# Holding the tensor engine's instructions to the order of the file, in a two-layer trunk on one Trainium2 core

## The chip, the core and the metric

The kernel runs on one core of a Trainium2 chip. The metric is the device time of one execution in microseconds (us). The engines are named as the profile names them: PE is TensorE (PEld its weight loads), DVE is VectorE, ACT is ScalarE, POOL is GpSimd, and SP is the engine that issues the transfers. PEclk is the clock that TensorE was granted, as a share of 2.4 GHz.

## What is computed

A trunk of two layers over 256 positions of width 1024. Layer 0 mixes tokens by dilated attention (16 heads of 64, three key groups), layer 1 by an mLSTM block (inner width 2048, four heads, two chunks of 128). Each layer also has a squared-ReLU MLP and a gated per-layer embedding. Cut to what matters here:

```
# every layer i:
x += mixer_i(rms_norm(x));  x += W2 relu(W1 rms_norm(x))^2
x += sigmoid(rms_norm(x) @ W_g) * (p[i] @ W_p)
# layer 0: q, k = rms_norm(q), rms_norm(k) per head, before the scores
# layer 1, per head: the running maximum m, then
s   = (q @ k.T) * exp(d_mat - m_t)
num = sc * (q @ C) + s @ v
den = sc * (q @ n) + sum(s)
h   = num / max(|den|, exp(-m_t))      # then an RMS norm of h over the head
```

## The kernel before

The activations live in SBUF with features on the partitions and the 256 positions along the free axis. All large weights are streamed from HBM once, as units of 1 MB (`raw`, three buffers). ACT rounds each chunk of 512 columns to `hi` (line 180, in `split`), DVE forms `lo = raw - hi` (line 181), and a product in full precision is three matmuls on PE: high by high, low by high, high by low. In the attention's projections (`qkv_block`, lines 487 to 519) these have 512 columns (lines 503 to 505), in `stream` (lines 335 to 337) 256.

The program is written against a clock of slots, four to a unit. `open_slot` and `close_slot` frame a slot's matmuls, 12 of them in either kind of stage, which is what a later step's due time counts in. `at(slot, f)` puts small work (norms, transposes, scores, the mLSTM's per-head steps) behind the matmuls of a slot. That is the order of the file. The framework's scheduler may reorder what stands in it on each engine: it takes, of the instructions that its own model holds to be ready, the one of highest priority, so that a matmul whose input that model holds to be late is put back and others go ahead of it. Each engine then executes its list strictly in order.

The places that matter:

- `qkv_block`: a block of queries and keys takes 8 slots, two halves (`b` is the half of the positions) of eight k-steps each. Behind it `qk_stats` (a reduction, line 438) and `qk_norm` (lines 442 to 447) run on DVE: a reciprocal root of some ten small dependent instructions (`rsqrt`, lines 285 to 289), then two wide products into `nqk` (line 447). `TQ` slots later `qk_turn` transposes `nqk` on PE (line 455).
- `first_stats` (added at slot 0) computes the very first norm's statistics, `rx`, with another `rsqrt` on DVE; `Stats.total` forms `ssum` (line 273) and sums it over partitions on PE (line 276).
- `small_products` (lines 405 to 424): at slot 44 a transfer on SP brings `rep` (in the buffer `pj`), and POOL forms small products of weights from it (lines 415 to 421), used much later in the mLSTM.
- `spread` (lines 291 to 298): DVE writes a diagonal `dg` from a column (line 295), PE multiplies it by ones (line 297), ACT copies the result (line 298).
- the mLSTM's per-head steps, at slots that `HS` and `HO` set (line 203): `decay`, `memory`, `factor` and `merge`. `factor` (lines 900 to 913) sums `s1` (shown as `s`) on PE (line 903), runs 14 small dependent DVE instructions (lines 905 to 908 and 285 to 289), and calls `spread`, whose `dg` PE needs. `memory` of the next head needs `p`, which `decay` makes on DVE (lines 870 and 871). `merge` (lines 915 to 926) is wide work on DVE.
- `scores` (lines 522 to 537) issues the products of two heads pairwise into two PSUM buffers; DVE's reduction of a buffer (line 544) frees it.

Of the kernel before, what the change touches and what calls it, by code (L numbers as in the profile page):

```python
# [18 lines left out]
D, S, P = 1024, 256, 128  # L19
# [113 lines left out]
def build(tc, a):  # L133
    nc = tc.nc
    ctx = ExitStack()
    with ctx:
        _build(ctx, tc, nc, a)


def _build(ctx, tc, nc, a):  # L140
# [16 lines left out]

    act = nc.scalar.activation
    dve = nc.vector
    mm = nc.tensor.matmul  # L160


    raw, hi, lo = {}, {}, {}
# [39 lines left out]
    GT, HS, HO = (4, 6, 7), (6, 12, 18, 24), (0, 2, 5, 7)  # L203
    ST0 = 3.5
    ST1 = 1
    TQ = 4

    TA = (12, 7)

    def at(slot, f, *args):  # L210
        fill.setdefault(slot, []).append((f, args))
# [19 lines left out]
    ident = base.tile([P, P], F32, name="ident")  # L231
# [17 lines left out]
    def pr(n):  # L249
        o, w = PCOL[n]  # L250
        return prm[:, o:o + w]
# [31 lines left out]
    def rsqrt(y, v, shape):  # L283
        t = sqp.tile(shape, F32, name="rt")
        dve.tensor_scalar(y.bitcast(I32), v.bitcast(I32), -0.5, RSQRT_MAGIC, op0=ALU.mult, op1=ALU.add)
        for _ in range(3):
            dve.tensor_tensor(t, y, y, op=ALU.mult)
            dve.scalar_tensor_tensor(t, t, -0.5, v, op0=ALU.mult, op1=ALU.mult)
            dve.scalar_tensor_tensor(y, t, 1.5, y, op0=ALU.add, op1=ALU.mult)
# [88 lines left out]
    def first_stats():  # L378
        st.total()
        sw = atp.tile([P, P], F32, name="sw")  # L380
        dve.tensor_copy(sw[:, 0:64], st.s[:, 192:256])
        dve.tensor_copy(sw[:, 64:128], st.s[:, 0:64])
        for n, t in ((2, st.s[:, 64:192]), (3, sw)):
            mm(st.ps[:, 256 + n:257 + n], t, ones[:, 0:1], start=True, stop=True)
        v = atp.tile([P, 4], F32, name="v4")
        dve.tensor_scalar(v, st.ps[:, 256:260], 1.0 / D, EPS, op0=ALU.mult, op1=ALU.add)
        dve.tensor_scalar(epsx, v[:, 0:2], EPS, None, op0=ALU.mult)
        rsqrt(rx, v, [P, 4])
# [3 lines left out]
            act(hW[n][:, :, 0:64], hA[n][:, :, 192:256], AF.Copy)  # L392
            act(hW[n][:, :, 64:128], hA[n][:, :, 0:64], AF.Copy)

    at(0, first_stats)
    at(8, wrap)


# [1 line left out]
    rep = pj.rearrange("p a b -> p (a b)")[:, 0:NR]  # L400
# [2 lines left out]
    wgM = base.tile([P, 16, 8], F32, name="wgM")  # L403

    def small_products():
        nc.sync.dma_start(rep, a["rep"])
        wq, wk, wv = (pr(n).rearrange("p (k j) -> p k j", j=4) for n in ("wq", "wk", "wv"))
        t2 = atp.tile([P, 16, 8], F32, name="t2")

        def contract(out, w, name, n, add=None):  # L410
            o, c = RCOL[name]
            r = rep[:, o:o + c].rearrange("p (k n j) -> p k n j", n=n, j=4)
            t = atp.tile([P, 16, 8, 4], F32, name="ct")[:, :, :n]
            for k in range(0, 16, 8):
                nc.gpsimd.tensor_tensor(t[:, k:k + 8], w[:, k:k + 8, None, :].to_broadcast([P, 8, n, 4]),
                                        r[:, k:k + 8], op=ALU.mult)
            for j in range(2):
                nc.gpsimd.tensor_tensor(t[:, :, :, j], t[:, :, :, j], t[:, :, :, j + 2], op=ALU.add)
            nc.gpsimd.tensor_tensor(out, t[:, :, :, 0], t[:, :, :, 1], op=ALU.add)
            if add is not None:  # L420
                nc.gpsimd.tensor_tensor(add, add, out, op=ALU.add)

        for n, c in enumerate(((mcomp, wq, "wkr", 4), (wgX, wq, "g0", 8), (t2, wk, "g1", 8, wgX), (wgM, wv, "g2", 8))):
            at(clock[0] + 4 * n + 1, contract, *c)
# [4 lines left out]
    QT, KTt, VT = {}, {}, {}  # L429
# [10 lines left out]
    def qk_norm(accs):  # L440
        v = atp.tile([P, 2, 8], F32, name="vqk", bufs=2)
        dve.scalar_tensor_tensor(v, STAT["ss"], 1.0 / HD, epsx[:, :, None].to_broadcast([P, 2, 8]), op0=ALU.mult, op1=ALU.add)
        f = atp.tile([P, 2, 8], F32, name="fqk", bufs=2)
        rsqrt(f, v, [P, 2, 8])
        n = atp.tile([P, 2, 512], F32, name="nqk")
        for b in range(2):
            dve.tensor_tensor(n[:, b].rearrange("p (h d) -> p h d", d=HD), accs[b].rearrange("p (h d) -> p h d", d=HD),
                              f[:, b, :, None].to_broadcast([P, 8, HD]), op=ALU.mult)
        return n

    def qk_turn(qt, g, ty, n):
        ps = pst.tile([P, 2, S], F32, name="tp")
        for pair in range(2):
            for b in range(2):
                nc.tensor.transpose(ps[:, pair, b * P:(b + 1) * P], n[:, b, ty * 256 + pair * P:ty * 256 + (pair + 1) * P], ident)  # L455
        t = [atp.tile([P, 2, S], F32R if g == 0 else F32, name=f"t{ty}{g}{n}", bufs=2) for n in ("hl" if g == 0 else "h")]
        if ty == 0:
            act(t[0], ps, AF.Copy)
            if g == 0:
                dve.tensor_tensor(t[1], ps, t[0], op=ALU.subtract)  # L460
        else:
            for pair in range(2):
                c = 2 * qt + pair
                act(t[0][:, pair], ps[:, pair], AF.Copy, scale=kgain[:, g, c:c + 1])
                if g == 0:
                    dve.scalar_tensor_tensor(t[1][:, pair], ps[:, pair], kgain[:, g, c:c + 1], t[0][:, pair],
                                             op0=ALU.mult, op1=ALU.subtract)
        (QT if ty == 0 else KTt)[qt, g] = t
# [18 lines left out]
    def qkv_block(qt, what, g):  # L487

        u0 = clock[0] // 4
        accs = []  # L490
        for i in range(8):
            open_slot()
            for j in (2 * i, 2 * i + 1):
                b, k = divmod(j, 8)
                if k == 0:
                    pl, nm = (pss, "sc") if qt == 0 and g == 0 and what == "qk" and b == 0 else (psa, "acc")
                    accs.append(pl.tile([P, 512], F32, name=nm))
                wh, wl = weights(u0 + k // 4, k % 4 * 512, 512)
                if (what, g) == ("v", 2):
                    hh, hl = (t[:, k] for t in hW) if b else (t[:, k, 64:192] for t in hA)  # L500
                else:
                    hh, hl = (t[:, k, b * P:(b + 1) * P] for t in hA)
                mm(accs[b], hh, wh, start=(k == 0), stop=False)  # L503
                mm(accs[b], hh, wl, start=False, stop=False)  # L504
                mm(accs[b], hl, wh, start=False, stop=(k == 7))  # L505
                if k == 7:
                    if what == "qk":
                        qk_stats(b, accs[b])
                    elif g == 0:
                        v_out(qt, 0, b, accs[b][:, 0:256])  # L510
                        v_out(qt, 1, b, accs[b][:, 256:512])
                    else:
                        v_out(qt, 2, b, accs[b][:, 0:256])
                        v_out(qt + 1, 2, b, accs[b][:, 256:512])
            if i == 7 and what == "qk":
                n = qk_norm(accs)
                for ty in range(2):
                    at(clock[0] + TQ + ty, qk_turn, qt, g, ty, n)
            close_slot()
# [29 lines left out]
    def turn(qt, i):  # L549
        pe, m = INST[qt, i]  # L550
        dve.reciprocal(m[:, 3:4], m[:, 2:3])
        dve.tensor_scalar(pe, pe, m[:, 3:4], None, op0=ALU.mult)
        ps = pst.tile([P, 2, S], F32, name="tp")
        psf = ps.rearrange("p a b -> p (a b)")[:, 0:SC]
        for k in range(3):
            nc.tensor.transpose(psf[:, k * P:(k + 1) * P], pe[:, k * P:(k + 1) * P], ident)  # L556
        pt = atp.tile([P, SC], F32, name="pt", bufs=4)
        act(pt, psf, AF.Copy)
        INST[qt, i] = pt
# [238 lines left out]
    ai = lp.tile([P, 2, 4], F32, name="ai")  # L798
    em = lp.tile([P, 2, 4], F32, name="em")
    Mrow = lp.tile([4, S], F32, name="Mrow")  # L800
# [36 lines left out]
    def gates_c():  # L837
        ps = SMALL["ps"]
        for b in range(2):
            nc.tensor.transpose(ps[0:4, 16 + b * P:16 + (b + 1) * P], ai[:, b], ident)  # L840
        arow = lp.tile([4, S], F32, name="arow")
        dve.tensor_copy(arow, ps[0:4, 16:16 + S])
        dve.tensor_tensor_scan(Mrow, arow, arow, -3e38, ALU.max, ALU.max)

    def gates_d():
        ps = SMALL["ps"]
        for b in range(2):
            nc.tensor.transpose(ps[:, 300 + 4 * b:304 + 4 * b], Mrow[:, b * P:(b + 1) * P], ident[0:4, 0:4])
        mt = gt("mt")
        dve.tensor_tensor(mt.rearrange("p b h -> p (b h)"), ps[:, 300:308],  # L850
                          SMALL["bs"].rearrange("p b h -> p (b h)"), op=ALU.add)
        act(em, mt, AF.Exp, scale=-1.0)
# [226 lines left out]
```

## Time and profile before

| what | value |
|---|---|
| time, median of 3 runs | 910.12 us (909.98 to 912.25) |
| the profiled execution's own time | 912.26 us |
| its span | 910.5 us |
| PE busy | 894.8 us (98%), 6924 instructions |
| DVE busy | 659.2 us (72%) |
| ACT busy | 568.5 us (62%) |
| POOL busy | 39.4 us (4%) |
| HBM traffic | 164 GB/s over the span |
| mean granted clock of PE | 0.997 |
| chain that ended last | PE 92%, DVE 6%, issue 1%, ACT 1% |

The span counts from the first instruction to the last of one execution; the time of an execution is a little longer. Busy time of PE counts matmuls whose ends are modelled, and a matmul may overlap its neighbours in the records, so what one costs is read from the distance between starts. Waits are told by the line that waited and what released it.

### The profile page before, as it was taken

Reading aid. Unit: us, or ns where it says so; the run is one execution under the profiler, and the core shown is the slowest. Engines: PE = TensorE matmul, PEld = TensorE weight load, DVE = VectorE, ACT = ScalarE, POOL = GpSimd, SP = SyncE. Lnnn points to the kernel's source line nnn. Section 1 sums busy time; section 2 is a strip of 40 time slices with the busy share of each in tenths; the row PEclk is TensorE's granted clock in tenths of the full one; section 3 lists DMA queues with packets and bytes.
Section 4 is the critical chain, followed back from the end, with each engine's and each line's share of the span. In section 5 each row is a group of like instructions: output and inputs, shape, how many; then the busy total and the mean of one; then the engine's idle time right before and its main releaser. Section 6 shows DMA issues by size and latency. Waiting matters only on the chain.

```text
span 910.5 us, 17609 instructions
## 1 busy us (share of the span) xinstructions
PE 894.8 (98%) x6924; PEld 833.9 (92%) x6924; DVE 659.2 (72%) x1409; ACT 568.5 (62%) x1055; POOL 39.4 (4%) x77
## 2 busy tenths in 40 slices
PE   8799999999999999999999999999999999999997
PEld 7687787777889999999999989999999999999997
DVE  6966877857876977765666987668898766656664
ACT  7567576676675766655555777678766666655552
POOL 0410000000000000000000343000000000000000
PEclk9999999999999999999999999999999999999999
DMA  8744434445343455555555433442256555555521
GB/s 305 282 140 147 178 130 150 143 141 180 132 148 137 149 188 185 190 183 188 187 191 175 154 130 134 140 140 93 94 197 223 175 187 188 188 183 188 190 102 47
DMA packets 23122, 150.23 MB, mean 165 GB/s; under 512 B 2560, under 2 KB 3200, under 8 KB 5632
## 3 DMA queue, kind: packets, MB, share of 16 engines
q1 hardware_dynamic: 23040, 149.12, 47.4%
q8 instruction: 54, 0.88, 0.4%
q14 instruction: 28, 0.23, 0.1%
HBM read 148.06 MB, written 1.05 MB: 164 GB/s over the span
## 4 chain that ended last, share of the span: by engine, by line
PE 92%; DVE 6%; issue 1%; ACT 1%; DMA 0%; SPq 0%; ACTq 0%
PE acc L335 21%; PE acc L336 21%; PE acc L337 20%; PE acc L503 6%; PE acc L505 6%; PE acc L504 6%; DVE lo L181 2%; PE tp L455 1%; PE tp L556 1%; PE sm L574 1%; PE sc L531 1%; PE tp L745 1%; PE tp L755 1%; PE sc L886 1%; PE sc L763 1%
## 5 line engine op out<-in xcount | busy, mean ns | idle before, releaser
L181 DVE TENSOR_TENSOR lo<-raw,hi 128x512 fp32r<-128x512 f32 x552 | 375.3, 690 | 169.2 <-ACT hi L180 163.8
L180 ACT ACTIVATE hi<-raw 128x512 fp32r<-128x512 f32 x552 | 338.7, 628 | 216.8 <-PE acc L336 194.1
L335 PE MATMUL acc<-hh,hi 128*128 128x256 f32 x640 | 182.5, 285 | 0.2 <-ACT hh L302 0.2
L336 PE MATMUL acc<-hl,hi 128*128 128x256 f32 x640 | 179.8, 281 | 0.4 <-DVE hl L303 0.3
L337 PE MATMUL acc<-hh,lo 128*128 128x256 f32 x640 | 179.7, 281 | 0.0
L337 PE MATMUL acc<-hidh,lo 128*128 128x256 f32 x512 | 143.3, 280 | 0.0
L336 PE MATMUL acc<-hidl,hi 128*128 128x256 f32 x512 | 143.3, 280 | 0.0
L335 PE MATMUL acc<-hidh,hi 128*128 128x256 f32 x512 | 143.1, 279 | 0.0
L336 PEld LDWEIGHTS acc<-hl,hi 128*128 128x128 f32 x640 | 121.7, 190 | 1.0 <-DVE hl L303 0.8
L335 PEld LDWEIGHTS acc<-hh,hi 128*128 128x128 f32 x640 | 120.7, 189 | 1.5 <-issue 0.7
L337 PEld LDWEIGHTS acc<-hh,lo 128*128 128x128 f32 x640 | 120.3, 188 | 0.0
L503 PE MATMUL acc<-hi,hh 128*128 128x512 f32 x264 | 109.9, 417 | 0.0
L504 PE MATMUL acc<-lo,hh 128*128 128x512 f32 x264 | 104.4, 396 | 0.8 <-DVE lo L181 0.8
L505 PE MATMUL acc<-hi,hl 128*128 128x512 f32 x264 | 104.8, 397 | 0.0
L336 PEld LDWEIGHTS acc<-hidl,hi 128*128 128x128 f32 x512 | 96.3, 188 | 0.0
L335 PEld LDWEIGHTS acc<-hidh,hi 128*128 128x128 f32 x512 | 96.2, 188 | 0.0
L337 PEld LDWEIGHTS acc<-hidh,lo 128*128 128x128 f32 x512 | 96.0, 188 | 0.0
L336 PE MATMUL acc<-hBl,hi 128*128 128x256 f32 x320 | 89.9, 281 | 0.0
L335 PE MATMUL acc<-hBh,hi 128*128 128x256 f32 x320 | 89.8, 281 | 0.0
L337 PE MATMUL acc<-hBh,lo 128*128 128x256 f32 x320 | 89.5, 280 | 0.0
L335 PEld LDWEIGHTS acc<-hBh,hi 128*128 128x128 f32 x320 | 60.3, 188 | 0.3 <-issue 0.3
L336 PEld LDWEIGHTS acc<-hBl,hi 128*128 128x128 f32 x320 | 60.1, 188 | 0.0
(258 smaller groups left out, 1382.7 us busy)
## 6 DMA issues: line engine op xcount, KB each, us to landing
raw<-w SPq DMA_DIRECT2D x136, 1024.0 KB, 4.9
raw<-w SPq DMA_DIRECT2D x8, 256.0 KB, 5.9
x<-x SPq DMA_DIRECT2D x4, 256.0 KB, 5.6
pj<-rep SPq DMA_DIRECT2D x1, 896.0 KB, 6.7
out<-u SPq DMA_DIRECT2D x3, 256.0 KB, 2.4
pT<-p SPq DMA_DIRECT2D x2, 256.0 KB, 3.9
nd<-nd SPq DMA_DIRECT2D x1, 384.0 KB, 5.6
out<-u SPq DMA_DIRECT2D x2, 128.0 KB, 1.9
```

The source lines that it names most:

```text
L180: act(hi[n][:, d], raw[u][:, s], AF.Copy)
L181: dve.tensor_tensor(lo[n][:, d], raw[u][:, s], hi[n][:, d], op=ALU.subtract)
L335: mm(acc[:, q], wh, h, start=first, stop=False, skip_group_check=n > 1)
L336: mm(acc[:, q], wh, l, start=False, stop=False, skip_group_check=n > 1)
L337: mm(acc[:, q], wl, h, start=False, stop=last, skip_group_check=n > 1)
L455: nc.tensor.transpose(ps[:, pair, b * P:(b + 1) * P], n[:, b, ty * 256 + pair * P:ty * 256 + (pair + 1) * P], ident)
L503: mm(accs[b], hh, wh, start=(k == 0), stop=False)
L504: mm(accs[b], hh, wl, start=False, stop=False)
L505: mm(accs[b], hl, wh, start=False, stop=(k == 7))
L531: mm(ps[:, 0:256], q[r, pair, tb], k[r, pair], start=first, stop=last)
L556: nc.tensor.transpose(psf[:, k * P:(k + 1) * P], pe[:, k * P:(k + 1) * P], ident)
L574: mm(out, VT[qt, 0][:, n, cols], pt[:, n * P:(n + 1) * P], start=(n == 0), stop=False, skip_group_check=True)
```

## The change

Every matmul and every transpose now goes through `tc.keep_in_program_order`: each PE instruction is held behind the one written before it, so PE's list is the order of the file, and the scheduler can place only the other engines' work. (In the changed kernel all PE instructions carry the lines of the two wrappers, 164 and 167, and other lines have moved by 7 to 11.) Four further edits:

- the first block of queries and keys goes through both halves of the positions in turn at each k-step, where it took half 0 and then half 1;
- `first_stats` is traced at the end of that first block, not at slot 0;
- `TQ` is 5 instead of 4: the transposes of `nqk` come one slot later;
- `small_products` begins with a one-column POOL copy from the first value tile into `rep`, so that the transfer into `rep` and the POOL products behind it wait for the first values.

```diff
-    mm = nc.tensor.matmul
+    def mm(*args, **k):
+        return tc.keep_in_program_order(nc.tensor.matmul(*args, **k))
+
+    def transpose(*args):
+        return tc.keep_in_program_order(nc.tensor.transpose(*args))
...
-    TQ = 4
+    TQ = 5
...
-    at(0, first_stats)
...
     def small_products():
+        nc.gpsimd.tensor_copy(rep[:, 0:1], VT[0, 0][:, 0, 0:1])
         nc.sync.dma_start(rep, a["rep"])
...
-                b, k = divmod(j, 8)
+                k, b = divmod(j, 2) if u0 == 0 else divmod(j, 8)[::-1]
...
             if i == 7 and what == "qk":
+                if u0 == 0:
+                    first_stats()
                 n = qk_norm(accs)
...
# and transpose(...) for nc.tensor.transpose(...) at its four places
```

What moves, at the two places that the prediction dwells on. First PE around the first head's `factor` in the mLSTM. `sm<-ones,s` are its sums, `sm<-dg,ones` is `spread`'s matmul, `acc` rows are the streamed products. Before, the sums stand here:

```order
L336 MATMUL acc<-hl,hi 128x256
L337 MATMUL acc<-hh,lo 128x256
L903 MATMUL sm<-ones,s_7529 128x1 x2
L335 MATMUL acc<-hh,hi 128x256
L336 MATMUL acc<-hl,hi 128x256
```

and, with 35 rows of streamed products between, `spread`'s matmul:

```order
L337 MATMUL acc<-hh,lo 128x256
L335 MATMUL acc<-hh,hi 128x256
L297 MATMUL sm<-dg,ones 128x128 x2
L336 MATMUL acc<-hl,hi 128x256
L337 MATMUL acc<-hh,lo 128x256
L886 MATMUL sc<-p,V 128x256
```

With the change they stand one behind the other, at all four heads:

```order
L164 MATMUL acc<-hl,hi 128x256
L164 MATMUL acc<-hh,lo 128x256
L164 MATMUL sm<-ones,s_7530 128x1 x2
L164 MATMUL sm<-dg,ones 128x128 x2
L164 MATMUL acc<-hh,hi 128x256
L164 MATMUL acc<-hl,hi 128x256
```

No streamed product is left between the sums and the matmul that needs their result. DVE's list between the two, at the first head, is with the change (`dd` and `vv` are the denominator and the variance, `ff` and `rt` the reciprocal root):

```order
L916 SCALAR_TENSOR_TENSOR dd<-sm,em 128x2
L188 TENSOR_TENSOR lo<-raw,hi 128x512
L917 TENSOR_TENSOR dd<-sm,dd 128x2
L188 TENSOR_TENSOR lo<-raw,hi 128x512
L918 SCALAR_TENSOR_TENSOR dd<-dd 128x2
L188 TENSOR_TENSOR lo<-raw,hi 128x512
L919 SCALAR_TENSOR_TENSOR vv<-sm,dd 128x2
L292 TENSOR_SCALAR ff<-vv 128x2
L294 TENSOR_TENSOR rt<-ff 128x2
```

Nine more small rows follow, and then `dg`: the chain is 14 small instructions long and has three wide splits in it (at the other heads two, one and two wide rows).

Second, DVE at the end of the first block's norm, the last rows before `nqk`. Before:

```order
L181 TENSOR_TENSOR lo<-raw,hi 128x512
L288 SCALAR_TENSOR_TENSOR rt<-rt,vqk 128x16
L181 TENSOR_TENSOR lo<-raw,hi 128x512
L289 SCALAR_TENSOR_TENSOR fqk<-rt,fqk 128x16
L438 TENSOR_REDUCE ss<-sqh 128x8
L447 TENSOR_TENSOR nqk<-sc,fqk 128x512
L447 TENSOR_TENSOR nqk<-acc,fqk 128x512
```

With the change:

```order
L188 TENSOR_TENSOR lo<-raw,hi 128x512
L295 SCALAR_TENSOR_TENSOR rt<-rt,v_311 128x4
L295 SCALAR_TENSOR_TENSOR rt<-rt,vqk 128x16
L188 TENSOR_TENSOR lo<-raw,hi 128x512
L296 SCALAR_TENSOR_TENSOR rx<-rt,rx 128x4
L296 SCALAR_TENSOR_TENSOR fqk<-rt,fqk 128x16
L188 TENSOR_TENSOR lo<-raw,hi 128x512
L294 TENSOR_TENSOR rt<-fqk 128x16
L446 TENSOR_REDUCE ss<-sqh 128x8
```

Two reciprocal roots (`rx` of `first_stats`, `fqk` of the block) now go side by side; from the reduction ahead of the block's chain to the second `nqk` DVE's list has 15 wide rows and 20 small ones, where before it had 13 and 11. On PE the transposes that need `nqk` stand 30 matmuls behind the first block, where before 39 stood in between.

## Rows read from the trace of the kernel before

**Rows 1.** The page, busy time of each engine.
```profile
PE 894.8 (98%) x6924; PEld 833.9 (92%) x6924; DVE 659.2 (72%) x1409; ACT 568.5 (62%) x1055; POOL 39.4 (4%) x77
```

**Rows 2.** Waits of PE: total us, times, longest.
```profile
PE tp L455 <- DVE nqk L447: 4.9, 1, 4.9
PE sm L297 <- DVE dg L295: 1.6, 1, 1.6
...
PE tp L861 <- DVE Mrow L843: 0.3, 1, 0.3
```

**Rows 3.** Windows of 1 us: length, busy time and count of PE, PEld, DVE, ACT, POOL; PEclk, DMA share, GB/s.
```profile
45.00:46.00 1.00, 1.00 (x4) 0.74 (x3) 0.14 (x1) 0.00 (x0) 1.00 (x3) 0.50 0.53 205
...
48.00:49.00 1.00, 1.00 (x7) 0.90 (x6) 0.05 (x1) 0.71 (x2) 0.21 (x1) 0.90 0.00 0
...
526.00:527.00 1.00, 1.00 (x11) 1.00 (x10) 0.58 (x2) 0.61 (x2) 0.00 (x0) 1.00 0.85 303
```

**Rows 4.** Timeline of DVE around the stall and a block later: start, us, line, form.
```profile
38.15 0.70 DVE L287 TENSOR_TENSOR rt<-fqk 128x16 f32<-128x16 f32 x1
38.77 0.68 DVE L181 TENSOR_TENSOR lo<-raw,hi 128x512 fp32r<-128x512 f32 x1
...
56.00 0.18 DVE L287 TENSOR_TENSOR rt<-fqk 128x16 f32<-128x16 f32 x1
```

**Rows 5.** Timeline of POOL, first and last of its 13 groups between them.
```profile
34.59 1.12 POOL L415 TENSOR_TENSOR ct<-prm,pj 128x128 f32<-128x128 f32 x2 [34.14 <-DMA pj<-rep]
...
47.48 0.73 POOL L419 TENSOR_TENSOR wgM<-ct 128x128 f32<-128x128 f32 x1
```

**Rows 6.** Timeline of DVE, the first block's norm.
```profile
21.91 0.68 DVE L438 TENSOR_REDUCE ss<-sqh 128x8 f32<-128x512 f32 x1
...
29.02 0.17 DVE L289 SCALAR_TENSOR_TENSOR fqk<-rt,fqk 128x16 f32<-128x16 f32 x1
29.10 0.68 DVE L438 TENSOR_REDUCE ss<-sqh 128x8 f32<-128x512 f32 x1
...
30.30 0.68 DVE L447 TENSOR_TENSOR nqk<-acc,fqk 128x512 f32<-128x512 f32 x1
```

**Rows 7.** Timeline of PE, neighbouring matmuls of 512 columns.
```profile
49.05 0.39 PE L505 MATMUL acc<-hi,hl 128*128 128x512 f32 x1
49.28 0.40 PE L503 MATMUL acc<-hi,hh 128*128 128x512 f32 x1
```

**Rows 8.** A window of 100 us in layer 1, columns as in Rows 3.
```profile
700.00:800.00 100.00, 100.00 (x852) 100.00 (x851) 70.40 (x111) 61.54 (x105) 0.00 (x0) 1.00 0.53 181
```

**Rows 9.** Timelines of DVE and PE at the norm's sums, first MLP.
```profile
308.29 0.42 DVE L273 TENSOR_TENSOR ssum<-sqa 128x256 f32<-128x256 f32 x1
...
308.77 0.38 PE L276 MATMUL sm<-ones,ssum 128*128 128x1 f32 x2
```

**Rows 10.** The same at the mLSTM's norm.
```profile
516.53 0.41 DVE L273 TENSOR_TENSOR ssum<-sqa 128x256 f32<-128x256 f32 x1
...
517.06 0.43 PE L276 MATMUL sm<-ones,ssum 128*128 128x1 f32 x3
```

**Rows 11.** Timelines of PE and DVE, the first head's factor and merge.
```profile
616.54 0.50 PE L903 MATMUL sm<-ones,s 128*128 128x1 f32 x4
...
619.52 0.16 DVE L285 TENSOR_SCALAR ff<-vv 128x2 int32<-128x2 int32 x1
...
621.54 0.48 DVE L295 TENSOR_SCALAR dg<-ident,ff 128x128 f32<-128x128 f32 x2
...
621.89 0.49 PE L297 MATMUL sm<-dg,ones 128*128 128x128 f32 x2
...
623.08 1.28 DVE L922 TENSOR_TENSOR mt<-mt,fb 128x512 f32<-128x512 f32 x2
```

**Rows 12.** Timeline of PE, scores of the last quarter; the first is of an earlier turn.
```profile
265.06 0.39 PE L531 MATMUL sc<-t10h,t00h 64*128 64x256 f32 x2
...
269.67 0.38 PE L531 MATMUL sc<-t10h,t00h 64*128 64x256 f32 x1
...
270.60 0.39 PE L335 MATMUL acc<-oTh,hi 128*128 128x256 f32 x1
270.91 0.38 PE L531 MATMUL sc<-t10h,t00h 64*128 64x256 f32 x1
...
271.84 0.39 PE L336 MATMUL acc<-oTl,hi 128*128 128x256 f32 x1
```

**Rows 13.** Timeline of DVE, the reduction that frees a scores buffer.
```profile
269.77 0.56 DVE L544 CUSTOM_DVE_ANT_0 scs<-sc,nd 128x384 f32<-128x384 f32 x1 [0.51 <-PE tp L556]
```

More of the change, by code (lines that the diff above doesn't have):

```diff
@@ L454, in qk_turn @@
             for b in range(2):
-                nc.tensor.transpose(ps[:, pair, b * P:(b + 1) * P], n[:, b, ty * 256 + pair * P:ty * 256 + (pair + 1) * P], ident)
+                transpose(ps[:, pair, b * P:(b + 1) * P], n[:, b, ty * 256 + pair * P:ty * 256 + (pair + 1) * P], ident)
         t = [atp.tile([P, 2, S], F32R if g == 0 else F32, name=f"t{ty}{g}{n}", bufs=2) for n in ("hl" if g == 0 else "h")]
@@ L555, in turn @@
         for k in range(3):
-            nc.tensor.transpose(psf[:, k * P:(k + 1) * P], pe[:, k * P:(k + 1) * P], ident)
+            transpose(psf[:, k * P:(k + 1) * P], pe[:, k * P:(k + 1) * P], ident)
         pt = atp.tile([P, SC], F32, name="pt", bufs=4)
@@ L839, in gates_c @@
         for b in range(2):
-            nc.tensor.transpose(ps[0:4, 16 + b * P:16 + (b + 1) * P], ai[:, b], ident)
+            transpose(ps[0:4, 16 + b * P:16 + (b + 1) * P], ai[:, b], ident)
         arow = lp.tile([4, S], F32, name="arow")
@@ L847, in gates_d @@
         for b in range(2):
-            nc.tensor.transpose(ps[:, 300 + 4 * b:304 + 4 * b], Mrow[:, b * P:(b + 1) * P], ident[0:4, 0:4])
+            transpose(ps[:, 300 + 4 * b:304 + 4 * b], Mrow[:, b * P:(b + 1) * P], ident[0:4, 0:4])
         mt = gt("mt")
```

## The prediction

> **What bounds the kernel now.** I read the busy times first [rows 1]: PE is busy for 98% of the span, every other engine for 72% or less. The chain that ended last says the same (PE 92%). So the change can gain only what PE loses in waits and in its clock, and anything that makes PE stand is paid in full: no other engine has work that could catch up for it. Next come the waits of PE [rows 2]. One is large, 4.9 us at the transposes of `nqk`; one is 1.6, at a `dg` of the mLSTM's input; the other that matters below is 0.3. All the waits of PE together are some 10 us. The change's upper gain is therefore small, and the question is how many new waits the order of the file brings. For these I went through the places where PE's list changes and asked, at each, how late the result is that PE now meets sooner.
>
> A difference of about 0.3% (2.7 us) is what a measurement of this kernel can tell from no change.
>
> **The sum**, against the profiled execution's own 912.26 us, which stands 2.14 above the median of the runs, 910.12.
>
> *The big wait.* The stall at 44.69 comes from a reciprocal root on DVE that ran while POOL worked. A small instruction of it took 0.70 us then and 0.18 in the next block, while the wide split beside it took 0.68 [rows 4]; POOL was busy from 34.59 to 48.21 [rows 5]. With the change POOL starts only after the first values, about 30 us later, and the transposes have 30 matmuls ahead of them. At the later block's 0.18 a step [rows 4] its eleven steps and the few wide rows around them fit into those 6.9 us. Gain 4.95. Behind the stall PE ran at 0.50 of its clock, that is at 1.2 GHz, in the windows from 45 to 48, and at 0.90 in the windows on either side [rows 3]: 3 x 0.5 + 2 x 0.1 = 1.7 lost, which goes too. Together **-6.65**.
>
> *The first block.* Its two halves now end together, its root shares DVE with that of `first_stats`, and its transposes stand 30 matmuls behind it. Before, 13 wide and 11 small rows took from 21.91 to 30.98 [rows 6], just covered by 39 matmuls of 0.23 [rows 7]. A wide row costs 0.60, a small one between two splits 0.08 (29.02 to 29.10). Now 15 x 0.60 + 20 x 0.08 = 10.6 stand against 30 x 0.23 = 6.9: PE waits 3.6, and 0.4 more for the splits that this makes late. **+4.0** (3.4 to 4.5).
>
> *POOL's new place.* Its 13.6 us of work fall on the first scores. A small DVE instruction there can be stretched by up to 0.5 [rows 4], but the wide ones are not, and the steps have about half a us to spare. **+0.8** (0 to 2). The transfer of `rep` is issued later on SP, with the next unit's weights behind it not due yet: nothing.
>
> *Norm sums that come sooner.* In the first MLP `ssum` ended at 308.71 and PE took it at 308.77 [rows 9]; in the mLSTM's norm 516.94 and 517.06 [rows 10]. Both were just in time. Now PE's sums stand 12 and 24 streamed matmuls sooner. These cost 100/852 = 0.117 each [rows 8], so PE waits **+1.4** and **+2.8**. The 1.6 at `dg` [rows 2] moves along with them. The transposes of `Mrow`, already 0.3 late [rows 2], come 13 matmuls sooner: **+1.5**. Each of the three is at least nothing, if DVE does the work sooner too, and at most this.
>
> *The factor of each head*, the largest term. PE's sums started at 616.54 and take their result's way through 14 small DVE instructions, `dg` and the matmul on it [rows 11]. Ten steps, from 619.52 to 621.54, are 2.02, so 0.20 a step. From the start of the sums: 0.50 for them, 14 x 0.20 = 2.8 to `dg`, 0.35 from `dg` to its matmul: 3.65, of which 0.36 is PE's own time for the sums. Some 3.3 is what PE must stand at the least, since nothing else is between. A wide split in the chain makes a step 0.66 long instead of 0.20: 0.46 each, three at the first head, two, one and two at the others. And the first instruction finds DVE busy with a split, 0.2 on average (0 to 0.6). That is 4.9 + 4.4 + 4.0 + 4.4 = **+17.7** (13.2 to 20). Before, 35 rows of streamed matmuls covered it. Streamed work is not lost, but it now stands behind the wait.
>
> *The next head's memory.* Its `p` stands behind the merge on DVE. From `dg` on PE to the first merge row it is 623.08 - 621.89 = 1.2 [rows 11]; then come six wide rows, a wide result, a split, and `w` and `p`, 5.7 in all. PE has 36 matmuls, the `dg` matmul and `decay`'s, 5.5. At 1.4 for each of three heads: **+4.2** (0 to 5).
>
> *Gains of the order.* The scores of two heads run beside each other when issued in pairs, and two turns of the last quarter were issued one head at a time, 269.67 to 270.60 and 270.91 to 271.84 [rows 12]. In pairs, PE waits for the reduction that frees the second buffer (to about 270.3, [rows 13]) and then needs 0.93 once: 0.45 sooner, twice, **-0.9**. Seven more changes between the streamed and the plain products go away; one turn costs 270.91 - 270.60 - 0.12 = 0.19 [rows 12]: **-1.3**.
>
> The sum: -6.65 + 4.0 + 0.8 + 1.4 + 2.8 + 1.5 + 17.7 + 4.2 - 0.9 - 1.3 = +23.55.
>
> *The clock.* A stand of 4.95 us was followed by the lower level, a loss of 1.7; one of 1.6, before 525.55, was not, the clock being 1.00 right behind it [rows 2, 3]. The first head's 4.9 is like the former, the other heads' 4.0 to 4.4 and the first block's 3.6 lie between. I take one fall, +1.7. In all **+25.25**: 937.5 for the profiled execution, and with the median 910.12 + 25.25 = **935.4**.
>
> The Trainium skill, on the page "TensorE: Matmul & The Clock Gate" (Part 1, The HAM clock gate), says that an array that has stood idle is throttled to half its clock and only sustained activity lifts that again. By that rule every one of the five long stands could be followed by a slow stretch; the trace agrees as far as its 4.95 us stand goes, and has none between that and 1.6.
>
> **Rivals.**
>
> *Every long stand lowers the clock.* Three more heads and the first block, each up to 1.7: 4 x 1.7 = 6.8 on top, with POOL's upper bound up to 943. For it: the stands are of nearly one length. Against: the level fell once in the whole trace, behind the longest stand.
>
> *POOL costs at its new place what it cost at the old one.* The scores' own small instructions are stretched as the reciprocal root's was, and PE stands 4.95 there again: 935.4 + 4.95 - 0.8 = 939.6. For it: the same 13.6 us of POOL work. Against: a turn of the scores has only a few small instructions, the root eleven in a row. The Trainium skill, on the page "GPSIMD Engine Reference" (section 1, Specifications), says that GpSimd shares its SBUF interfaces with VectorE and contends with instructions that have two SBUF inputs. By that rule the wide splits, with two inputs, would be stretched too, and this rival would be the likelier; here the split's 0.68 in the midst of POOL's work speaks against it.
>
> *The lesser waits are absorbed.* While PE stands at one place DVE works on, so that at the next it is ahead. Then the norm sums and `Mrow` cost half (-2.85), POOL nothing (-0.8), `memory` half (-2.1), the factors their minimum (-4.5) and the clock nothing (-1.7): 935.4 - 11.95 = 923, and half of that way 929. For it: DVE has 28% to spare. Against: the places follow one another's results, and DVE's spare time lies elsewhere.
>
> *Faster.* The file's order is good, and every pinned instruction finds its result: only the gains and the first block stay, -6.65 + 4.0 - 0.9 - 1.3 = -4.85, 905. It would take that the chain behind a head's sums is done when PE reaches `dg`. The point that decides is the wait there: under about 1 us a head (4 us in all, with the lesser waits gone) the gain wins. The rows speak against it: 14 dependent instructions cannot take less than 2.8.
>
> *No difference.* The call that holds the order might do nothing, or only at a few places; then the scheduler still moves matmuls ahead of late ones and the gain of the first block's region is all but eaten by its own wait: 908 to 912. The list of the built kernel speaks against it: PE's rows there follow the file.
>
> **How the numbers follow.** My own case, 929 to 939, has 0.54; the clock falling at all stands, 939 to 943, 0.16; POOL's old cost at its new place, about 939.6, 0.04; the lesser waits absorbed, 923 to 929, 0.16; faster, 0.04; no difference, 0.03; something slower that I have not seen, above 943, 0.03. The range leaves out the last three and the lower half of the absorbed case, 0.18 together: 926 to 943. Chances: faster 0.04, within 0.3% 0.03, slower 0.93.
>
> **What would show it.** In the profile after, the waits of PE should have no large `nqk` wait in the second block and one of about 3.6 in the first; `sm` waiting for `dg` should stand five times, four of 4 to 5 us between 610 and 690; `sm` on `p` three times 1.4; `ssum` 1.4 and 2.8. PEclk should be 1.00 from 44 to 48, and 0.50 somewhere behind the first head's factor. POOL should be busy from about 64 to 78. I am wrong if the factors' waits are under 3 us each, which would mean that DVE's chain is shorter than its rows, or if the waits are as I say and the time is not longer by their sum, which would mean that PE was not the bound there.

## The result, and the profile after

The changed kernel takes 942.67 us (median of 4 runs, 942.12 to 942.97), the kernel before 910.05 (909.96 to 912.25): a ratio of 1.0355, with a 95% interval of 1.034 to 1.0371. It is 32.6 us slower by the medians, and 29.86 by the two profiled executions (942.12 against 912.26). Span and busy times of the changed kernel, from its page:

```profile
span 940.3 us, 17617 instructions
...
PE 900.9 (96%) x6924; PEld 838.0 (89%) x6924; DVE 664.0 (71%) x1409; ACT 571.0 (61%) x1055; POOL 37.7 (4%) x78
```

Against [rows 1] the other engines' busy times differ by less than 5 us. PE is busy for 6.1 us more (900.9 - 894.8) with the same number of instructions. Its waits, total us, times and the longest:

```profile
PE sm L164 <- DVE dg L302: 16.8, 4, 4.8
PE sm L164 <- DVE ssum L280: 5.7, 2, 4.2
PE tp L167 <- DVE nqk L455: 3.1, 2, 2.8
PE sm L164 <- DVE p L881: 2.0, 3, 1.0
PE tp L164 <- DVE Mrow L854: 1.8, 1, 1.8
...
PE tp L167 <- DVE m L562: 0.8, 1, 0.8
PE sc L164 <- DVE m L555: 0.7, 2, 0.3
```

With the smaller lines all waits are 34.7 us, where the list of before summed up to 10.7 [rows 2 has its main lines]. So 24.0 us of new waits and 6.1 of longer busy time, 30.1 together, are nearly the 29.8 by which the span grew. The new waits stand at the places that the prediction named. The 6.1 I read as the slow stretches of PE's clock, less some work that the order saved; the second part is worked out below and not shown by a run of its own. These are seven windows of 1 us, one from each slow stretch that the trace has between the start and the end (columns as in [rows 3], PEclk is the third from the end):

```profile
35.00:36.00 1.00, 1.00 (x4) 0.70 (x4) 0.93 (x2) 0.39 (x2) 0.00 (x0) 0.50 0.93 375
516.00:517.00 1.00, 1.00 (x7) 1.00 (x7) 1.00 (x3) 0.00 (x0) 0.73 (x2) 0.50 0.76 106
609.00:610.00 1.00, 1.00 (x7) 1.00 (x7) 0.00 (x0) 0.98 (x3) 0.00 (x0) 0.50 0.00 0
627.00:628.00 1.00, 1.00 (x6) 1.00 (x6) 0.83 (x2) 0.14 (x1) 0.00 (x0) 0.50 0.14 57
646.00:647.00 1.00, 1.00 (x6) 1.00 (x6) 0.00 (x0) 0.18 (x1) 0.00 (x0) 0.50 0.00 0
667.00:668.00 1.00, 1.00 (x7) 1.00 (x7) 1.00 (x2) 0.00 (x0) 0.00 (x0) 0.50 0.02 8
687.00:688.00 1.00, 1.00 (x6) 1.00 (x6) 1.00 (x2) 0.00 (x0) 0.00 (x0) 0.50 0.00 0
```

PE is busy throughout. In the six windows of layer 1 it has six or seven matmuls, where the window at full clock in [rows 3] (526 to 527) has 11; the first window is in the projections, with matmuls twice as wide and transposes. Before, one such stretch stood in the trace [rows 3]. PE's timeline shows what stands ahead of them and how slow they are:

```profile
514.96 0.60 PE L164 MATMUL sm<-ones,ssum 128*128 128x1 f32 x4 [4.25 <-DVE ssum L280]
...
607.43 0.75 PE L164 MATMUL tp<-Mrow,ident 4*128 4x256 f32 x2 [1.76 <-DVE Mrow L854]
...
620.18 0.50 PE L164 MATMUL sm<-ones,s 128*128 128x1 f32 x4
...
625.50 1.22 PE L164 MATMUL sm<-dg,ones 128*128 128x128 f32 x4 [4.81 <-DVE dg L302]
...
685.30 1.22 PE L164 MATMUL sm<-dg,ones 128*128 128x128 f32 x4 [4.07 <-DVE dg L302]
...
686.96 0.41 PE L164 MATMUL acc<-hBh,hi 128*128 128x256 f32 x1
687.17 0.41 PE L164 MATMUL acc<-hBl,hi 128*128 128x256 f32 x1
```

A streamed matmul takes 0.21 us behind the stand (686.96 to 687.17), where it cost 0.117 [rows 8]. DVE's chain between sums and `dg` at the first head is the one that was counted, three wide splits in it:

```profile
620.99 0.15 DVE L916 SCALAR_TENSOR_TENSOR dd<-sm,em 128x2 f32<-128x2 f32 x1
621.06 0.68 DVE L188 TENSOR_TENSOR lo<-raw,hi 128x512 fp32r<-128x512 f32 x1
621.66 0.15 DVE L917 TENSOR_TENSOR dd<-sm,dd 128x2 f32<-128x2 f32 x1
...
625.16 0.48 DVE L302 TENSOR_SCALAR dg<-ident,ff 128x128 f32<-128x128 f32 x2
```

A step with a split in it is 0.67 long (620.99 to 621.66). From the start of the sums to the `dg` matmul it is 625.50 - 620.18 = 5.32. In [rows 11] the same two instructions of PE were 5.35 apart (616.54 to 621.89) and PE worked all that time.

### The profile page after: what moved, and what is told of

Read it like the earlier page. It is cut to its first block, busy times and chain, and to the rows that moved or that the text cites. A ratio compares the mean times of both kernels' runs of the same rounds, so it can differ in the third digit from the quotient of the medians.

```text
span 940.3 us, 17617 instructions
## 1 busy us (share of the span) xinstructions
PE 900.9 (96%) x6924; PEld 838.0 (89%) x6924; DVE 664.0 (71%) x1409; ACT 571.0 (61%) x1055; POOL 37.7 (4%) x78
## 4 chain that ended last, share of the span: by engine, by line
PE 87%; DVE 9%; ACT 1%; issue 1%; DMA 1%; SPq 0%; ACTq 0%
PE acc L164 76%; PE sc L164 4%; PE sm L164 3%; DVE lo L188 3%; PE tp L167 2%; PE tp L164 1%; DMA raw<-w 1%; DVE hl L310 1%; DVE xn L712 0%; DVE mt L933 0%; DVE sqa L275 0%; DVE mt L934 0%; DVE u L687 0%; DVE scs L555 0%; DVE y L795 0%
## 5 line engine op out<-in xcount | busy, mean ns | idle before, releaser
L164 PEld LDWEIGHTS acc<-hh,hi 128*128 128x128 f32 x640 | 123.2, 193 | 1.3 <-issue 1.0
L164 PEld LDWEIGHTS acc<-hh,lo 128*128 128x128 f32 x640 | 122.5, 191 | 0.0
```

The lines of the kernel that those rows point to most:

```text
L164: return tc.keep_in_program_order(nc.tensor.matmul(*args, **k))
```

## The experiments

The runs below come from other chips than the result, so each is given as a ratio to the kernel before on its own chip. A ratio of 0.001 is 0.9 us.

**Which part of the change costs: the edits without the held order.**

```diff
-        return tc.keep_in_program_order(nc.tensor.matmul(*args, **k))
+        return nc.tensor.matmul(*args, **k)
```

(and the same for the transposes)

> The changed kernel with all its edits but the hold on the order. Theory (the loss is new stands of PE that the held order brings, and its low clock behind them; the other edits only take the 4.95 us wait of the second block away): near 906 us, 904 to 909, with the waits on dg, Mrow and p of the kernel before. Rival (the other edits cost, POOL's work on the first scores and the norm that comes later): 930 to 943. Either way the 4.95 us wait at nqk should be gone.

Measured: 0.9967 (0.9949 to 0.9984), 910.83 against 913.24, so 3 us faster than before; on the 910.05 of the first chip that would be some 907. The theory stands: without the held order the other edits cost nothing in all. One thing was not expected. The wait at the second block went down, but not away. It has moved from the transposes to a matmul of the third block, which needs a PSUM buffer that `nqk` still reads:

```profile
PE acc L164 <- DVE nqk L455: 2.7, 1, 2.7
...
45.00:46.00 1.00, 1.00 (x4) 0.81 (x4) 0.69 (x1) 0.60 (x1) 0.00 (x0) 0.50 0.00 0
```

The second line is a window behind that wait, which ended at 42.43: the clock is at 0.50.

**The held order without the other edits.** The kernel before with the two wrappers alone.

```diff
-    mm = nc.tensor.matmul
+    def mm(*args, **k):
+        return tc.keep_in_program_order(nc.tensor.matmul(*args, **k))
```

(and a wrapper for the transposes)

> The kernel before with the held order alone, none of the other edits. Theory: all the stands of the changed kernel's mLSTM part (dg 16.8 us, Mrow 1.8, ssum 5.7, p 2.0 and the low clock behind them), and in the first blocks two waits at nqk of some 4 to 6 us, since 24 matmuls and not 30 stand ahead of the transposes and POOL works beside the second: 945 to 952 us. Rival (the other edits cost): 910 to 916. A second rival (each held instruction costs a little at its issue, everywhere): about 943 without large waits in the list.

Measured: 1.0397 (1.0373 to 1.0421), 949.01 us. Time as expected, place only in part:

```profile
PE sm L161 <- DVE dg L299: 16.8, 4, 4.8
PE sm L161 <- DVE ssum L277: 12.0, 3, 6.3
```

The 16.8 at `dg` is there to the tenth. The waits at `nqk` are 2.2 us, not the 8 to 12 that I expected; ahead of them PE stands 6.3 us for the very first norm's sums, which the order of the file puts ahead of the stream. Why so little was left at `nqk` was not tested. That is what the later `first_stats` of the change is for once the order is held: with it this stand is not in the list.

**The order held only through the projections.**

```diff
     lead[0] = LS
+    pin[0] = False
```

(the wrappers hold an instruction only while `pin[0]` is set)

> The changed kernel, its order held only to the end of the projections and first attention turns (36 of some 136 units), free from there on. Theory: the waits behind that stage are those of the kernel before, the first block keeps its wait of about 3 us and its slow stretch of 1.7 lost, the 4.95 us wait is gone: 908 to 912 us. Rival of a cost at each held instruction: 910 plus a quarter of the 33 us, about 918. Rival of the other edits: 935 to 943.

Measured: 0.9994 (0.9978 to 1.0011), 912.73 against 913.24: no difference, as expected. The first block keeps a wait of 2.8 us at `nqk`, and the mLSTM has the waits of before. A cost of each held instruction as such, which would have given about 1.009, is excluded for this stage. So the loss lies behind the projections, and in the order there.

**The clock apart from the waits: PE kept busy during the four long stands.**

```diff
+        fl = pst.tile([P, 2, S], F32, name="tp")
+        for _ in range(15):
+            mm(fl[:, 0, 0:128], ones, ones, start=True, stop=True)
```

(in `factor`, behind the sums)

> The changed kernel with 15 small matmuls of ones (128 columns, into a PSUM buffer that nobody reads) between the sums and the dg matmul of each of the four heads: PE still cannot go on before dg stands, but it is busy for most of the wait. Theory (a stand is followed by a slow stretch, which costs over and above the stand): the granted clock stays at 1.00 behind the four factors, and the time falls by the 7.2 us that these stretches take from busy PE (1.5 + 1.7 + 1.7 + 2.3): 935 to 936.5 us. Rival (the low level in the records costs nothing, DVE's chain alone sets the time): 942 to 943. If the fill outlasts the chain, the time rises by what it is longer.

Measured: 1.0267 (1.0238 to 1.0295), 937.14 us, against 1.0355 for the changed kernel: 8.0 us less, for an expected 7.2. PE's timeline at the first head, and the granted clock behind it:

```profile
624.11 0.50 PE L164 MATMUL sm<-ones,s 128*128 128x1 f32 x4
624.47 3.60 PE L164 MATMUL tp<-ones 128*128 128x128 f32 x30
628.94 0.71 PE L164 MATMUL sm<-dg,ones 128*128 128x128 f32 x4 [0.87 <-DVE dg L302]
...
642.21 0.50 PE L164 MATMUL sm<-ones,s 128*128 128x1 f32 x4
```

```profile
629.00:630.00 1.00, 1.00 (x9) 1.00 (x10) 0.08 (x1) 0.32 (x1) 0.00 (x0) 1.00 1.00 426
630.00:631.00 1.00, 1.00 (x11) 0.87 (x9) 0.90 (x2) 0.07 (x2) 0.00 (x0) 1.00 0.49 197
```

From the sums to the `dg` matmul it is 4.83 us here and 5.32 in the changed kernel, the chain having one split less at this head; at the other three the distances are the same to 0.02. So DVE's chain still sets when PE goes on. But the work behind it runs at 1.00, at all four heads. How much time that gives back can be read from the traces. In the changed kernel the next head's sums stand here:

```profile
640.97 0.50 PE L164 MATMUL sm<-ones,s 128*128 128x1 f32 x4
```

From the first head's `dg` matmul to them are 15.47 us there (625.50 to 640.97) and 13.27 here (628.94 to 642.21). Behind the second and third head it is 15.66 and 15.15 against 13.50 and 13.42, and from the last head's `dg` matmul to the end 255.0 against 253.0. That is 8.1 us less in all for the same work. The waits on `p`, 0.4 us here and 2.0 there, are 1.6 of it; the other 6.5 are the slow stretches, which so cost time over and above the stands. The 8.0 of the two ratios, each known to some 0.003 or 2.7 us, fits with that, but it is the weaker evidence: in this profiled execution the clock also fell elsewhere, to 0.50 from 8 to 11 and from 32 to 38 us, where the changed kernel's trace has one stretch, around 35 to 37. The first head's sums so come 3.9 us later, and the two spans differ by 4.7 only.

**POOL alone.** The kernel before with one line:

```diff
     def small_products():
+        nc.gpsimd.tensor_copy(rep[:, 0:1], VT[0, 0][:, 0, 0:1])
```

> The kernel before with one edit alone: POOL's small products wait for the first values; no held order, nothing else moved. Theory (POOL's work beside the second block's reciprocal root made the 4.95 us wait): the small DVE rows there fall from 0.70 to 0.17 us, the wait at nqk shrinks to under 3 us (what the run without the held order still had there) and the time falls by 2 to 5 us, ratio 0.995 to 0.998. Rival (the wait came from the order of DVE's list, not from POOL): wait unchanged near 5 us, ratio 1.000.

Measured: 0.9974 (0.9957 to 0.9991), 910.32 against 912.41, 2 us faster. DVE's root in the second block, the waits, and the clock behind the stand:

```profile
41.76 0.18 DVE L287 TENSOR_TENSOR rt<-fqk 128x16 f32<-128x16 f32 x1
```

```profile
PE tp L456 <- DVE nqk L448: 2.8, 1, 2.8
```

```profile
43.00:44.00 1.00, 0.78 (x4) 0.69 (x5) 0.67 (x2) 0.00 (x0) 0.00 (x0) 1.00 0.95 401
44.00:45.00 1.00, 1.00 (x7) 0.84 (x6) 0.08 (x1) 0.74 (x2) 0.00 (x0) 1.00 0.16 66
```

The small instruction is back at 0.18, where [rows 4] have 0.70 beside POOL. That settles POOL's part: 2.1 of the 4.95 us were its doing. Four splits and a reduction still stand between the steps of the chain, which takes 5.26 us from its first step to `nqk` (37.12 to 42.38); in the changed kernel, with nothing between its steps, it takes 2.30 (42.34 to 44.64). But the splits alone do not make the wait: the run with POOL's line and the scores' buffers, below, has ten of them in the chain and a wait of 0.2 us. What makes the other 2.8 is that PE has no matmul with a free PSUM buffer to do meanwhile. The stand of 2.84 us was not followed by a slow stretch.

**POOL early in the changed kernel.** The changed kernel without that line.

> The changed kernel without POOL's wait: its products run from about 35 us on again, as before. Theory: the second block's reciprocal root is stretched again, eleven small steps by up to 0.5 each, less what its 30 matmuls leave free: a wait of 3 to 5 us at the second nqk and a slow stretch behind it come back, the waits of about 1.5 us on m in the first scores go: 2 to 6 us slower than the changed kernel, ratio to before 1.038 to 1.042. Rival (with 30 matmuls ahead the root has time enough in either case): the same as the changed kernel, 1.0355, or a little faster.

Measured: 1.0386 (1.0341 to 1.043), 947.97 us. A second wait at `nqk` is there:

```profile
PE tp L167 <- DVE nqk L454: 2.8, 1, 2.8
PE acc L164 <- DVE nqk L454: 2.3, 1, 2.3
```

The median moved as expected, but the interval includes the changed kernel's 1.0355, so no change in time is shown. The wait that returned is 2.3 us, less than the 3 to 5 expected, and no slow stretch stands behind it, which was expected too. Of the 1.5 on `m`, the 0.8 at the first scores is gone and the 0.7 at line 555's reduction is not: that one has nothing to do with POOL, it is the last quarter's pairs waiting for their second buffer. DVE's splits ahead of the first scores' `m` show what made the 0.8. In the changed kernel, beside POOL, and then here, without POOL:

```profile
74.48 1.16 DVE L188 TENSOR_TENSOR lo<-raw,hi 128x512 fp32r<-128x512 f32 x1
75.63 0.83 DVE L188 TENSOR_TENSOR lo<-raw,hi 128x512 fp32r<-128x512 f32 x1
...
76.43 0.68 DVE L188 TENSOR_TENSOR lo<-raw,hi 128x512 fp32r<-128x512 f32 x1
77.15 0.69 DVE L188 TENSOR_TENSOR lo<-raw,hi 128x512 fp32r<-128x512 f32 x1
```

The wide rows were stretched there, by 0.6 us together, and the small steps between them took 0.14 to 0.16 in both.

**The order held, but the late consumers written later in the file.**

```diff
+    def factor2(h):
+        HEAD[h]["fin"]()      # the dg matmul and the copy
...
-    ... HS, HO = ... (6, 12, 18, 24), (0, 2, 5, 7)
+    ... HS, HO = ... (7, 13, 19, 25), (0, 2, 5, 7, 7)
```

> The changed kernel with the order still held, but the late consumers written later in the file: the dg matmul of each head two slots behind its sums (24 streamed matmuls and one transpose between), and all heads one slot later. Theory (the loss is where the file puts the consumers, not the holding): the four dg waits fall from 16.8 us to 2 to 5, the slow stretches behind the four factors and behind Mrow go (7.2 + 1.7), the Mrow wait falls under 0.5; waits on p up to 3: 915 to 922 us, ratio to the kernel before 1.006 to 1.013. Rival (the holding itself costs, or DVE is the bound there): the waits move to p or to the merge, 930 or more.

Measured: 1.0155 (1.0119 to 1.019), 926.54 us: 18 us of the 32 come back, though less than expected. The order is held as before, so it is the place of the consumers in the file that costs. Most of what stays are these waits:

```profile
PE sm L164 <- DVE dg L302: 8.0, 4, 3.2
PE sm L164 <- DVE ssum L280: 5.7, 2, 4.2
```

The wait on `p` is gone, that on `Mrow` is 0.4. The `dg` waits are 8.0 where I expected 2 to 5: they are 0.7, 2.4, 1.8 and 3.2 at the four heads. DVE's list has more wide rows in the chain now, splits and at two heads the `w` and `p` of the next one, so that from the sums to the `dg` matmul it is 6.1 to 6.6 us at the last three heads, where it was 4.4 to 4.6 in the changed kernel; and the last head has no `decay` between. The slow stretches behind `Mrow` and behind three of the heads are gone, as expected. The one behind the last head's 3.2 is not, and a new one follows the 1.5 us stand at the first MLP's norm sums.

**A version that beats both.** The edits without the held order left 2.7 us at the second block, for a PSUM buffer. The scores' buffers are free until the first scores.

```diff
-                    pl, nm = (pss, "sc") if qt == 0 and g == 0 and what == "qk" and b == 0 else (psa, "acc")
+                    pl, nm = (pss, "sc") if qt == 0 and g < 2 and what == "qk" and b == 0 else (psa, "acc")
```

> All edits but the held order, and the second block's first half accumulates in the scores' PSUM buffers as the first block's does, so that the third block finds a free buffer and need not wait for nqk. Theory: the wait of 2.7 us at nqk and the slow stretch of 1.7 behind it go, 4.4 us less than without this edit: ratio to the kernel before 0.990 to 0.994. Rival: the wait returns at the transposes or at the scores, that now want the same buffers, and the ratio stays at 0.997.

Measured: 0.9929 (0.9906 to 0.9953), 906.54 against 912.41. Then the same line with only POOL's wait beside it, on the kernel before, and the former once more on the same chip:

> The kernel before with two edits alone: POOL's products wait for the first values, and the second block's first half accumulates in the scores' PSUM buffers. No held order, first norm, first block and TQ as before. Theory (the gain over the kernel before is the second block's wait alone, 2.84 us that were left with POOL out of the way, and what its slow stretch cost in the executions that had one): ratio to the kernel before 0.990 to 0.995, the same within 0.002 as the run that has all edits but the held order. Rival (the first block's alternate halves and the later first norm bring part of it): 0.996 to 0.998.

> The run of all edits but the held order with the scores' buffers, once more, beside the kernel with the two edits alone: 0.990 to 0.995 of the kernel before by the theory, and within 0.002 of that kernel.

Measured: 0.9932 (0.9907 to 0.9956), 904.11 us, for the two edits, and 0.9921 (0.9896 to 0.9945), 903.82 us, for all edits but the held order; the kernel before took 910.31. The two are the same. Two lines of the program bring the gain of 6 us (the scores' line without POOL's was not run). What is left of the wait in the run with the two edits, and where `nqk` is made there and in the run with POOL's line alone:

```profile
PE tp L456 <- DVE nqk L448: 0.2, 1, 0.2
...
44.83 0.68 DVE L448 TENSOR_TENSOR nqk<-sc,fqk 128x512 f32<-128x512 f32 x1
...
42.38 1.29 DVE L448 TENSOR_TENSOR nqk<-acc,fqk 128x512 f32<-128x512 f32 x2
```

`nqk` comes 2.45 us later here and PE still does not stand, since it does matmuls of the third block in the meantime.

## Why the prediction was right, and where it was short

The direction held, and so did the main mechanism: PE waits where the file puts consumers right behind their producers, 24.0 us of new waits by the list. That 942.67 lies in 926 to 943 is partly luck. It is 0.3 us under the upper end, above my own case of 929 to 939, and in the part that the range had from the rival with the clock; the forecast of 935.4 was 7.3 us short.

- *The big wait.* Predicted gone, and gone in the second block. Its cause was told half right: POOL made 2.1 of the 4.95, as the run with POOL alone shows. The rest stood there because PE had no matmul with a free PSUM buffer to do while DVE worked through the chain and its splits, as the run with the two edits shows. In the changed kernel no split stands in that chain, and it is done 1 us ahead of the transposes (45.93 to 46.96).
- *The first block.* 4.0 predicted, 3.1 measured, with a slow stretch behind it.
- *POOL's new place.* 0.8 predicted, and 0.8 measured: the wait of a transpose on `m` (L562) at 77.11 us, which is gone when POOL runs early. The number came true by another mechanism. The prediction let POOL stretch small instructions and said that the wide ones are not; here two wide splits took 1.16 and 0.83 us instead of 0.68, and the small steps were as short as without POOL. So its ground against the rival on POOL, the split's 0.68, does not hold in general either.
- *Norm sums.* 1.4 and 2.8 predicted, 5.7 together measured, 4.25 of it in the mLSTM's norm. Here the step "these cost 0.117 each" failed. The 24 matmuls that were passed over are not of the pitch of [rows 8] in the trace of before:

```profile
512.74 0.38 PE L335 MATMUL acc<-hh,hi 128*128 128x256 f32 x1
513.44 0.39 PE L336 MATMUL acc<-hl,hi 128*128 128x256 f32 x1 [0.32 <-DVE hl L303]
...
514.49 0.39 PE L335 MATMUL acc<-hh,hi 128*128 128x256 f32 x1 [0.20 <-ACT hh L302]
```

  They are the last 24 ahead of the sums at 517.06 [rows 10] and took 4.32 us (512.74 to 517.06) instead of 24 x 0.117 = 2.8, since some of them waited themselves for parts of the norm's input, as the rows show. The sums now wait for all of that at once. The wait of 1.6 at this norm's `dg` [rows 2], which I let stand, is not in the list after: the matmuls between run in the slow stretch, and DVE is done when they are.
- *Mrow.* Its wait was to grow by 1.5 from 0.3; it is 1.8.
- *The factors.* 17.7 predicted, 16.8 measured: 4.8, 4.1, 3.9 and 4.1 for the 4.9, 4.4, 4.0 and 4.4 that were worked out step by step.
- *The next heads' memory.* 4.2 predicted, 2.0 measured. One would think that the slow stretch behind `dg` gives DVE time to catch up, but in the run with the fill, where the clock stays up, the waits on `p` are smaller still (0.4, once). Why this term was too large stays open.
- *Gains of the order.* The pairs of scores wait 0.35 each for the reduction (0.7 on L555 in the list); the sum had a wait there too. The rest is not separated from the clock. PE's busy time grew by 6.1, and the seven slow stretches, by one minus the granted clock summed over the windows with PE busy, are 12.3 less the 1.7 of before, 10.6. An estimate from these: 10.6 - 6.1 = 4.5 us less work of PE, for the 2.2 that was predicted.
- *The clock* is the step that failed: "I take one fall, +1.7". There were seven, at all five long stands, at the mLSTM's norm sums and even behind the 1.76 us at `Mrow`. They cost 12.3 us where I took 1.7, some 10 us more. The run with the fill shows that cost by itself: with four stretches gone, the same work took 8.1 us less, 1.6 of it waits on `p`. The rival "every long stand lowers the clock", up to 943, was the case that came true, and I gave it 0.16. The rule that the Trainium skill has on the page "TensorE: Matmul & The Clock Gate" (Part 1), that an array which stood idle is throttled, would have given the better forecast of the clock. The trace of the changed kernel agrees with it at every long stand; the 2.84 us stand of the run with POOL alone was not followed by a slow stretch.

The terms of the waits alone, 27.45 predicted without the gains, stand against 24.0 measured. So against the profiled executions, +29.86 measured for +25.25 predicted, the clock was 10.6 short, and waits that were 3.4 too long and gains that were some 2.3 too small took more than half of that back. That the errors offset each other is luck.

A gain that the sum counted on may also not be in every execution. The sum took off the slow stretch of the profiled execution of before and applied the difference to the median, 2.14 us below it. Whether the median execution has that stretch no trace here shows; that the difference of the medians, 32.6, is some 2.8 larger than that of the profiled executions would fit with its having none.

## What to carry to other kernels

A list that a scheduler has loosened hides how late each result is: before holding an order, take each consumer that then moves up, and count the chain of instructions behind the producer that stands just ahead of it. Where the consumer stands right behind its producer, move it down in the file first, and look at what then comes into the chain of the producer; the held order as such cost nothing that could be measured over the projections. And on an engine that is busy for 98% of the time, price a wait of some microseconds with the slow stretch that may follow it (some 1.5 to 2.4 us each here), not by its length alone. Before all that, ask whether a free buffer would let the engine do other work during the wait: here one line for a PSUM buffer and one for POOL gained 6 us, and the held order lost 33.

## What the runs showed of the hardware that I had not expected

The length of a stand alone does not tell whether the clock falls behind it. A stand of 1.76 us at `Mrow` was followed by 0.50, one of 2.84 in the run with POOL alone was not, and one of 2.74 in the run without the held order was. Of two stands of 1.5 at the first MLP's norm sums, one was (the run with the later consumers) and one was not (the changed kernel). At the last head the clock fell in the midst of the stand (681.23 to 685.30), with PE idle, and that stretch lasted about twice as long as the others:

```profile
684.00:685.00 1.00, 0.00 (x0) 0.00 (x0) 0.82 (x6) 0.00 (x0) 0.00 (x0) 0.50 0.45 188
```

Such differences may be why executions of one kernel differ, the ten of the run without the held order between 905.47 and 912.41 us; only one of each kernel has a trace, so it is not shown.

And POOL's work did not stretch the same instructions of DVE each time. In the second block before, small ones grew fourfold (0.18 to 0.70) and most of the wide splits between them stayed at 0.68; at the first scores after, two wide splits grew to 1.16 and 0.83 and the small ones stayed. What decides between the two is not shown.
